# A layer with a 32-expert mixture on one core: expert results written from Pool's queue, token windows copied by VectorE one unit ahead, five experts instead of three with known addresses, four of them in pairs

## The chip, the core and the metric

The kernel runs on one core of a Trainium2 chip, as a single launch. The metric is the device time in microseconds (us) of that launch. A core has five engines that matter here: TensorE (PE in the rows, with its weight loads as PEld), VectorE (DVE), ScalarE (ACT), GpSimd (POOL) and SyncE (SP), which computes nothing and mainly issues DMAs. A q behind an engine's name (SPq, POOLq) is its sequencer, which waits, branches and issues. Each engine works through its own instructions in order and waits at semaphores for the others. DMAs move data between HBM and the on-chip memory; they run on 16 DMA engines that all queues share.

## What is computed

The reference is one layer over 512 latent tokens of width 1024: two mixers in parallel (a gated DeltaNet and a spatial gating MLP), an output projection with residual, and then the part that this change touches, a mixture of 32 experts. Each token picks one of four expert groups, and two of the eight experts in it:

```
p_group = jax.nn.softmax(t @ w_rg + b_rg)            # t: 512 tokens x 1024
grp = jnp.argmax(p_group, axis=-1)
logits_in = (t @ w_re + b_re) of the group grp       # 8 experts
top_p, top_i = lax.top_k(jax.nn.softmax(logits_in), 2)
...
hid = silu(t @ w1[e]) * (t @ w3[e])                   # 1024 x 256 each
out += (hid * gate[:, e]) @ w2[e]                     # 256 x 1024
```

The result is added to the residual and normalised. An expert has three parts of 1 MB each (float32, 128 x 2048): two hold w1 and w3, the third holds w2. All 32 experts are loaded, so 96 parts go through the DMA engines. There are 1024 assignments of a token to an expert, 32 for an expert in the mean. For the reference's inputs the router gives experts 0 to 4 these numbers of rows: 68, 9, 39, 31, 46; and the largest of the others 104, 94, 75, 65, 53, 47, 41, 35, 30.

## The kernel before, in words

The first 880 us compute the mixers and are not touched. Then come, for each block of 128 tokens, the output projection and the router's logits; `route` turns these into positions; `experts` runs the mixture; `combine` gathers each token's two results and writes the output.

**Routing.** `route` sorts the 1024 assignments by expert. It yields `off` (where an expert's rows begin), `count`, and a ranking of experts by count. Eight indirect DMAs on Pool's queue gather the token rows in that order (`xg`, 512 KB each, two in one buffer of 1 MB); TensorE transposes them into `xst` (ScalarE and VectorE copy the halves), 1024 columns of which are the sorted assignments. Of the experts, the first NS = 3 are taken by their number, so their addresses in HBM are known from the start. The other NR = 29 are taken by rank, the fullest first, and their addresses are read from `byi[0]`, which the ranking gives.

**Units.** `units` makes a list U. A unit is either one expert with a window of 128 columns of `xst`, or a pair of experts with 64 columns each; the two of a pair run side by side in TensorE, each on half of its columns. Before, U holds the three known experts singly, then the five largest singly, mixed with 12 pairs: 20 units. `unit_in` multiplies the window `exw` with w1 and w3 (`p<-eraw,exw`), forms `hid` with ScalarE and VectorE, and transposes it to `hT`. `unit_out` multiplies `hT` with w2 (`p<-eraw,hT`), VectorE scales the result into `ey`, and DMAs write its rows to `ysort` in HBM. They are issued in PIECES (rows 0 to 32 always, then 32 to 48, 48 to 64 and, for a single expert, 64 to 96 and 96 to 128 if the expert has as many rows).

**Conditional part.** A pair whose experts might have over 64 rows (ranks up to NB = 15) is followed by `second`: an `If` on all engines that repeats the unit for the rows past 64. There are five of them. The three parts of each of a pair's experts stay in their buffers until that `If` is done.

**Loads.** The list LOADS holds the parts in order of use: for each unit the first two parts of its experts, then the third parts of the unit before; the known experts come first. `load_parts(n)` issues loads on SP's queue up to number n. There are 16 buffers of 1 MB (8 in `er`, 8 in `er2`); the gathers `xg` use four of `er2`, so before routing at most 12 can be loaded. `route` is preceded by `load_parts(9)`, all that is known. Each buffer is used again when its part has been read.

**Queues.** SP issues, in order: the loads, the writes of `ey` pieces (L1198), and a register load for each condition (L1175). A DMA of one queue also waits until an earlier one, about eight DMAs back in the same queue, has landed. The window copy (L1152) stands on ScalarE just ahead of its `unit_in`. There are three `ey` buffers.

Of the kernel before, what the change touches and what calls it, by code (L numbers as in the profile page):

```python
# [9 lines left out]
F32 = mybir.dt.float32  # L10
F32R = mybir.dt.float32r
I32 = mybir.dt.int32
U32 = mybir.dt.uint32
AF = mybir.ActivationFunctionType
ALU = mybir.AluOpType
# [6 lines left out]
T = 512  # L22
# [8 lines left out]

NS, NB, NW = 3, 15, 5
NR = 32 - NS
NL = NR - NB
BASE = CAP * (NS + NB)
# [13 lines left out]
class K:  # L51
# [15 lines left out]
            mm(ps, wl(kt), xh(kt), start=False, stop=last and kt == kts - 1)  # L67


    ER, ER2, EY, HB = 8, 8, 3, 2  # L70

    PIECES, XL = ((0, 32), (32, 48), (48, 64), (64, 96), (96, 128)), (3,)

# [748 lines left out]
    def tail_mix(self, RM, R3):  # L822
# [58 lines left out]
        self.xst = self.xs.tile([128, KT, 2 * T + 64], F32, name="xst")  # L881
        R3.close()
        nc.gpsimd.memset(self.xst[:, :, 2 * T:], 0.0)
        self.load_parts(3 * NS)
        self.route(lg)

    def route_tiles(self):
# [31 lines left out]
    def route(self, lg):  # L919
# [116 lines left out]
        nc.gpsimd.tensor_tensor(end, self.off[0:1], win[0:1], op=SUB)  # L1036
        nc.gpsimd.tensor_tensor(end, end, self.count[0:1], op=ADD)
        nc.gpsimd.tensor_copy(self.cnti, end)
        by_rank(1, win[0:1, NS:])
        by_rank(2, end[:, NS:])  # L1040

# [24 lines left out]
    def moe_setup(self):  # L1066
        nc, c = self.nc, self.c
        BF = mybir.dt.bfloat16
        self.onesb = c.tile([128, 128], BF, name="onesb")
        nc.gpsimd.memset(self.onesb, 1.0)  # L1070
        self.lt = c.tile([128, 128], BF, name="lt")
        nc.gpsimd.affine_select(out=self.lt, in_=self.onesb, compare_op=ALU.is_gt, fill=0.0, base=0,
                                pattern=[[1, 128]], channel_multiplier=-1)

        self.tokn = c.tile([128, 2, 8], F32, name="tokn")
        for o, (pat, m) in enumerate((([[0, 8]], 1), ([[0, 2], [128, 4]], 0))):
            nc.gpsimd.iota(self.tokn[:, o], pattern=pat, base=0, channel_multiplier=m, allow_small_or_imprecise_dtypes=True)
        self.gate = c.tile([128, 2, 4], F32, name="gate")
        self.count = c.tile([128, 32], F32, name="count")
        self.off = c.tile([128, 32], F32, name="off")  # L1080
        self.offi = c.tile([1, 32], I32, name="offi")
        self.cnti = c.tile([1, 32], I32, name="cnti")
        self.byi = [c.tile([1, NR], I32, name=f"byi{i}") for i in range(3)]
        self.posi = c.tile([128, 8], I32, name="posi")
        self.tki = c.tile([128, 8], I32, name="tki")
        self.ysort = self.dp.tile([YROWS + 2 * T, D], F32, name="ysort")
# [22 lines left out]
    def units(self):  # L1109

        big = [(NS + r,) for r in range(NW)]
        small = [(NS + r, NS + r + 1) for r in range(NW, NR, 2)]
        self.U = [(e,) for e in range(NS)]
        while big or small:
            self.U += big[:1] + small[:2]
            big, small = big[1:], small[2:]

        ins = lambda u: [(e, k) for e in self.U[u] for k in range(2)]
        outs = lambda u: [(e, 2) for e in self.U[u]]
        self.LOADS = ins(0)  # L1120
        for u in range(1, len(self.U)):
            self.LOADS += ins(u) + outs(u - 1)
        self.LOADS += outs(len(self.U) - 1)
        self.LOADS.sort(key=lambda p: p[0] >= NS)
# [18 lines left out]
    def window(self, es, past=0):  # L1143

        nc = self.nc
        n = 128 // len(es)
        xw = self.eh.tile([128, KT, 128], F32, tag="exw", bufs=2, name="exw")
        for i, e in enumerate(es):
            src = self.offi[0:1, e:e + 1] if e < NS else self.byi[1][0:1, e - NS:e - NS + 1]
            o = nc.values_load(src, engines=(mybir.EngineType.Activation,), min_val=0, max_val=2 * T - 64,  # L1150
                               skip_runtime_bounds_check_because="the windows lie inside the tile")
            nc.scalar.copy(xw[:, :, n * i:n * i + n], self.xst[:, :, bass.ds(o + past, n)])  # L1152
        return xw

    def unit_in(self, es, w, xw):
# [17 lines left out]

    def rows_of(self, e):
        return self.nc.values_load(self.cnti[0:1, e:e + 1] if e < NS else self.byi[2][0:1, e - NS:e - NS + 1],  # L1175
                                   engines=(mybir.EngineType.SP,), min_val=0, max_val=2 * T,
                                   skip_runtime_bounds_check_because="an expert has at most T tokens")

    def unit_out(self, es, w2, hT, past=0):
        nc, ew = self.nc, self.ew  # L1180
        n = 128 // len(es)
        p2 = self.psm.tile([128, 2, 512], F32, tag="p2", bufs=2, name="p2")
        for h in range(2):
            for kt in range(2):
                for i in range(len(es)):
                    r = slice(n * i, n * i + n)
                    kw = {} if n == 128 else dict(tile_position=(0, n * i))
                    nc.tensor.matmul(p2[r, h, :], hT[:, kt, r], w2[i][:, kt, 512 * h:512 * h + 512],  # L1188
                                     start=kt == 0, stop=kt == 1, **kw)
        y = ew.tile([128, D], F32, tag="ey", bufs=self.EY, name="ey")  # L1190
        nc.vector.tensor_tensor(y, p2.rearrange("p a b -> p (a b)"), self.m5, op=MUL)  # L1191
        for i, e in enumerate(es):
            m = self.rows_of(e)
            row = CAP * e if e < NS + NB else BASE + 64 * (e - NS - NB)
            for a, b in self.PIECES:
                if past <= a < past + n:
                    kw = dict(cond=m > a) if a else {}
                    nc.sync.dma_start(self.ysort[row + a:row + b], y[n * i + a - past:n * i + b - past], **kw)  # L1198

    def second(self, es, w, w2):  # L1200

        src = self.byi[2][0:1, es[0] - NS:es[0] - NS + 1]
        m = self.nc.values_load(src, min_val=0, max_val=2 * T, skip_runtime_bounds_check_because="an expert has at most T tokens")
        with self.tc.If(m > 64):
            self.unit_out(es, w2, self.unit_in(es, w, self.window(es, 64)), 64)

    def experts(self):
        done, cur = 0, None
        for u in range(len(self.U) + 1):
            self.load_parts(done + self.ER + self.ER2)  # L1210
            last, cur = cur, None
            if u < len(self.U):
                es = self.U[u]
                w = [[self.eraw.pop((e, k)).rearrange("p (k c) -> p k c", k=4) for k in range(2)] for e in es]
                cur = es, w, self.unit_in(es, w, self.window(es) if u else self.xst[:, :, 0:128])
                done += 2 if len(es) == 1 else 0
            if last:
                es, w, hT = last
                w2 = [self.eraw.pop((e, 2)).rearrange("p (k c) -> p k c", k=2) for e in es]
                self.unit_out(es, w2, hT)  # L1220
                done += 1 if len(es) == 1 else 6
                if len(es) == 2 and es[0] < NS + NB:
                    self.second(es, w, w2)
# [270 lines left out]
```

## Time and profile before

| | us |
|---|---|
| three runs: median (lowest to highest) | 1249.03 (1247.0 to 1254.13) |
| the profiled execution, its own time | 1247.79 |
| its span, first to last instruction | 1246.1 |
| PE busy | 1055.2 (85%) |
| DVE busy | 593.1 (48%) |
| ACT busy | 429.6 (34%) |
| POOL busy | 218.8 (18%) |

The profiled execution lies 1.2 us below the median, and its span 1.7 us below its own time. The page's line of 40 slices shows PE at nine tenths over most of the span, at 4 tenths in the slice around the routing, and at nothing in the last. The DMA line reads 3 to 7 in the first two thirds and mostly 8 or 9 in the last third, where the experts are. To read the change, cut the span at 904 (routing), 924 (dynamic loads begin), 964, 1004 and 1204 us (the experts' end), and look in each stretch at what the DMA engines carry and at what SP's queue waits for.

### The profile page before, as it was taken

How to read it: one execution, taken by the hardware profiler on the slowest of the kernel's cores; microseconds unless marked ns; L12 is line 12 of the kernel's file. 1: busy time of each engine (PE TensorE's matmuls, PEld its weight loads, DVE VectorE, ACT ScalarE, POOL GpSimd, SP SyncE). 2: the span in 40 equal slices, each digit the busy share in tenths (PEclk: the TensorE clock that was granted, in tenths of full speed). 3: DMA queues.
4: the chain of work that ended last, by engine and by line, in shares of the span. 5: the costliest groups of instructions: out<-in, count | busy, mean ns of one | idle time of the engine just before them, and what ended most of it. 6: DMA issues, size and time to landing. Idle time of an engine off the chain costs nothing. (4 is left out here: it accounts for less than half of the span.)

```text
span 1246.1 us, 17491 instructions
## 1 busy us (share of the span) xinstructions
PE 1055.2 (85%) x6450; PEld 751.2 (60%) x6451; DVE 593.1 (48%) x1102; ACT 429.6 (34%) x850; POOL 218.8 (18%) x181
## 2 busy tenths in 40 slices
PE   4899878899798979988999999998859988889750
PEld 0577767787687768865677767887734332323210
DVE  5655774679365954585433434373571211111115
ACT  4656332754364535633235233242122001001002
POOL 2502111411141105111211011131150000000005
PEclk9999997899798989989999999998969998999985
DMA  9346652356322542336634457678569588999975
GB/s 372 94 155 230 185 181 57 106 137 236 85 97 79 172 115 86 90 115 189 237 105 149 154 172 267 199 235 319 213 225 412 201 325 350 376 367 400 406 297 219
DMA packets 108364, 262.01 MB, mean 210 GB/s; under 512 B 48400, under 2 KB 57072, under 8 KB 95600
## 3 DMA queue, kind: packets, MB, share of 16 engines
q1 hardware_dynamic: 99488, 238.45, 54.8%
q0 software_dynamic: 3456, 12.58, 2.7%
q10 hardware_dynamic: 5328, 9.77, 2.3%
q8 instruction: 54, 0.88, 0.3%
q14 instruction: 38, 0.31, 0.1%
HBM read 230.78 MB, written 47.30 MB: 223 GB/s over the span
## 5 line engine op out<-in xcount | busy, mean ns | idle before, releaser
L1163 PE MATMUL p<-eraw,exw 128*64 128x512 f32 (+1 forms) x496 | 150.5, 624 | 19.3 <-DMA eraw<-we 14.4
L63 PE MATMUL pcol<-xhi,wh 128*128 128x512 f32 x320 | 129.3, 404 | 3.5 <-ACT wh L121 3.2
L121 ACT CAST wh<-raw 128x1024 fp32r<-128x1024 f32 (+1 forms) x81 | 84.2, 1040 | 137.4 <-DMA raw<-win 34.1
L63 PE MATMUL pcol<-xhi,wl 128*128 128x512 f32 x320 | 128.4, 401 | 1.6 <-DVE wl L122 1.1
L63 PE MATMUL pcol<-xlo,wh 128*128 128x512 f32 x320 | 127.3, 398 | 0.0
L1163 PEld LDWEIGHTS p<-eraw,exw 128*64 128x64 f32 (+1 forms) x496 | 55.2, 155 | 104.5 <-issue 102.5
L122 POOL TENSOR_TENSOR wl<-raw,wh 128x1024 fp32r<-128x1024 f32 x27 | 65.7, 2434 | 276.2 <-ACT wh L121 216.1
L122 DVE TENSOR_TENSOR wl<-raw,wh 128x1024 fp32r<-128x1024 f32 (+1 forms) x54 | 66.6, 1233 | 58.5 <-ACT wh L121 50.8
L1188 PE MATMUL p<-eraw,hT 128*64 128x512 f32 (+1 forms) x256 | 84.5, 619 | 11.1 <-DMA eraw<-we 5.1
L63 PE MATMUL px<-xhi,wh 128*128 128x512 f32 x192 | 79.1, 412 | 9.4 <-DVE acc L349 6.5
L1165 ACT ACTIVATE hid<-p 128x256 f32<-128x256 f32 x20 | 7.7, 384 | 209.3 <-PE p L1163 206.8
L63 PE MATMUL px<-xhi,wl 128*128 128x512 f32 x192 | 77.4, 403 | 0.0
L63 PE MATMUL px<-xlo,wh 128*128 128x512 f32 x192 | 77.4, 403 | 0.0
L349 DVE SCALAR_TENSOR_TENSOR acc<-px,convw,acc 128x510 f32<-128x510 f32 (+1 forms) x96 | 71.4, 743 | 10.0 <-ACT acc L345 9.4
L63 PEld LDWEIGHTS pcol<-xhi,wh 128*128 128x128 f32 x320 | 60.8, 190 | 16.8 <-ACT wh L121 3.3
L63 PEld LDWEIGHTS pcol<-xhi,wl 128*128 128x128 f32 x320 | 60.8, 190 | 14.5 <-DVE wl L122 1.5
L63 PEld LDWEIGHTS pcol<-xlo,wh 128*128 128x128 f32 x320 | 61.1, 191 | 11.4
L1191 DVE TENSOR_TENSOR ey<-p,m5r 128x1024 f32<-128x1024 f32 x20 | 24.5, 1225 | 90.8 <-PE p L1188 60.6
L1166 DVE TENSOR_TENSOR hid<-hid,p 128x256 f32<-128x256 f32 x20 | 8.4, 421 | 115.1 <-ACT hid L1165 115.1
L1188 PEld LDWEIGHTS p<-eraw,hT 128*64 128x64 f32 (+1 forms) x256 | 27.3, 155 | 56.6 <-issue 46.1
L1321 POOL DMA_INDIRECT yk<-ysort,posi x8 | 8.2, 1019 | 288.5 <-SPq L1231 286.3
L483 DVE TENSOR_TENSOR xtmp<-X 112x30 f32<-112x30 f32 (+14 forms) x120 | 50.5, 421 | 11.4 <-POOL X L477 9.0
(394 smaller groups left out, 2171.2 us busy)
## 6 DMA issues: line engine op xcount, KB each, us to landing
eraw<-we SPq DMA_DIRECT2D x96, 1024.0 KB
raw<-win SPq DMA_DIRECT2D x64, 512.0 KB
adaw<-adaw SPq DMA_DIRECT2D x40, 512.0 KB
ysort<-wo SPq DMA_DIRECT2D x23, 512.0 KB
gr<-rowsd SPq DMA_DIRECT2D x8, 768.0 KB
ysort<-ey SPq DMA_DIRECT2D x48, 128.0 KB
adaw<-adaw POOLq DMA_DIRECT2D x8, 512.0 KB, 19.7
qd<-rowsd SPq DMA_DIRECT2D x8, 512.0 KB
```

The lines of the kernel that those rows point to most:

```text
L63: mm = lambda *a, **k: self.pace(self.nc.tensor.matmul(*a, **k))
L121: a = nc.scalar.copy(hi, src)
L122: b = (lo_eng or nc.vector).tensor_tensor(lo, src, hi.bitcast(F32), op=SUB)
L349: eng.scalar_tensor_tensor(acc[:, lo:hi], ps[:, lo + o:hi + o], w(d), acc[:, lo:hi], op0=MUL, op1=ADD)
L483: nc.vector.tensor_tensor(tv, bc(X[:, j + 1:, j], 2, j), bc(X[:, j, :j], 1, m), op=MUL)
L1163: nc.tensor.matmul(p13[r], xw[:, kt, r], w[i][kt // 4][:, kt % 4, :], start=kt == 0, stop=kt == KT - 1, **kw)
L1165: nc.scalar.activation(hid, p13[:, 0:256], AF.Silu)
L1166: nc.vector.tensor_tensor(hid, hid, p13[:, 256:512], op=MUL)
L1188: nc.tensor.matmul(p2[r, h, :], hT[:, kt, r], w2[i][:, kt, 512 * h:512 * h + 512], start=kt == 0, stop=kt == 1, **kw)
L1191: nc.vector.tensor_tensor(y, p2.rearrange("p a b -> p (a b)"), self.m5, op=MUL)
L1321: g = nc.gpsimd.indirect_dma_start(out=y[:, k, :], out_offset=None, in_=self.ysort, in_offset=bass.IndirectOffsetOnAxis(ap=self.posi[:, 4 ...
```

## The change

NS goes from 3 to 5, so 15 parts have known addresses. Experts 1 to 4 become two pairs, each followed by a conditional part, whose condition is the larger of the two counts (`mxi`, computed by VectorE). NR falls to 27, pairs by rank to 11; U has 19 units: 1 + 2 + 5 + 11, and there are seven conditional parts. `load_parts(12)` stands ahead of `route`. The writes of `ey` go from SP's queue to Pool's, with their register loads, and there are four `ey` buffers. The window copy goes from ScalarE to VectorE, and is issued for unit u + 1 behind `unit_in` of unit u.

```diff
-NS, NB, NW = 3, 15, 5
+NS, NB, NW = 5, 15, 5
-    ER, ER2, EY, HB = 8, 8, 3, 2
+    ER, ER2, EY, HB = 8, 8, 4, 2
...
-        self.load_parts(3 * NS)
+        self.load_parts(self.ER + self.ER2 - 4)
...
+        mx = rp.tile([1, NS - 1], F32, name="mxe")
+        nc.vector.tensor_tensor(mx, end[:, 0:NS - 1], end[:, 1:NS], op=ALU.max)
+        nc.vector.tensor_copy(self.mxi[:, 0:NS - 1], mx)
...
-        self.U = [(e,) for e in range(NS)]
+        self.U = [(0,)] + [(e, e + 1) for e in range(1, NS, 2)]
...
-            o = nc.values_load(src, engines=(mybir.EngineType.Activation,), min_val=0, max_val=2 * T - 64,
+            o = nc.values_load(src, engines=(mybir.EngineType.DVE,), min_val=0, max_val=2 * T - 64,
-            nc.scalar.copy(xw[:, :, n * i:n * i + n], self.xst[:, :, bass.ds(o + past, n)])
+            nc.vector.tensor_copy(xw[:, :, n * i:n * i + n], self.xst[:, :, bass.ds(o + past, n)])
...
-                                   engines=(mybir.EngineType.SP,), min_val=0, max_val=2 * T,
+                                   engines=(mybir.EngineType.Pool,), min_val=0, max_val=2 * T,
...
-                    nc.sync.dma_start(self.ysort[row + a:row + b], y[n * i + a - past:n * i + b - past], **kw)
+                    nc.gpsimd.dma_start(self.ysort[row + a:row + b], y[n * i + a - past:n * i + b - past], **kw)
...
-        src = self.byi[2][0:1, es[0] - NS:es[0] - NS + 1]
+        src = self.mxi[0:1, es[0]:es[0] + 1] if es[0] < NS else self.byi[2][0:1, es[0] - NS:es[0] - NS + 1]
...
-                cur = es, w, self.unit_in(es, w, self.window(es) if u else self.xst[:, :, 0:128])
+                cur = es, w, self.unit_in(es, w, xw)
+                if u + 1 < len(self.U):
+                    xw = self.window(self.U[u + 1])
```

SP's queue around the routing, before. L874 writes the rows that the gathers read; L1133 are loads with a known address, L1138 those with an address from the ranking:

```order
L1133 DMA eraw<-we 128x2048 x6
L874 DMA h2d<-x_7413 128x1024
L836 DMA x_7693<-x 128x1024
L874 DMA h2d<-x_7415 128x1024
L874 DMA h2d<-x_7417 128x1024
L1133 DMA eraw<-we 128x2048
L874 DMA h2d<-x_7693 128x1024
L1136 TENSOR_LOAD byi_103
L1138 ISA
L1138 DMA eraw<-we 128x2048
```

The same place now (a load with a known address is L1138, one by rank L1143):

```order
L1138 DMA eraw<-we 128x2048 x6
L874 DMA h2d<-x_7413 128x1024
L836 DMA x_7693<-x 128x1024
L874 DMA h2d<-x_7415 128x1024
L874 DMA h2d<-x_7417 128x1024
L1138 DMA eraw<-we 128x2048 x4
L874 DMA h2d<-x_7693 128x1024
L1138 DMA eraw<-we 128x2048 x3
L1141 TENSOR_LOAD byi_104
L1143 ISA
L1143 DMA eraw<-we 128x2048
```

Three more loads stand ahead of the last `h2d` write, and three more with known addresses ahead of the ranking's first use.

SP's queue in the middle of the experts, before: two loads of one unit, then the first of another unit's writes with the register load for their conditions.

```order
L1136 TENSOR_LOAD byi_103
L1138 ISA
L1138 DMA eraw<-we 128x2048
L1138 ISA
L1138 DMA eraw<-we 128x2048
L1198 DMA ysort<-ey 32x1024
L1175 TENSOR_LOAD byi_105
L1198 ISA
L1198 DMA ysort<-ey 16x1024
```

A load that comes later in this queue stands behind all of these writes. SP's queue around the first conditional part now (L1208 loads its condition, L1209 branches):

```order
L1143 DMA eraw<-we 128x2048
L1208 TENSOR_LOAD mxi
L1209 COMPARE_AND_BRANCH
L1209 UNCONDITIONAL_BRANCH x2
L1141 TENSOR_LOAD byi_104
L1143 ISA
L1143 DMA eraw<-we 128x2048
```

And Pool's queue for the second pair now, where before it held only the register loads and branches of the five conditional parts:

```order
L1203 DMA ysort<-ey 32x1024
L1180 TENSOR_LOAD cnti
L1203 ISA
L1203 DMA ysort<-ey 16x1024
L1203 ISA
L1203 DMA ysort<-ey 16x1024
L1203 DMA ysort<-ey 32x1024
L1180 TENSOR_LOAD cnti
L1203 ISA
L1203 DMA ysort<-ey 16x1024
```

The writes have left SP's queue altogether, body of the `If` included; between two loads there stands at most a register load and a branch.

## Rows read from the trace of the kernel before

**Rows 1.** Busy time by stretch: start:end, us, engines (x instructions), PEclk, DMA share, GB/s
```profile
core 0: us, PE busy (x) PEld busy (x) DVE busy (x) ACT busy (x) POOL busy (x), PEclk, DMA share, GB/s
904.00:916.00 12.00, 2.69 (x76) 2.40 (x76) 9.39 (x25) 1.70 (x5) 4.69 (x8) 0.50 0.11 45
924.00:964.00 40.00, 38.17 (x124) 19.98 (x123) 13.04 (x27) 9.85 (x15) 4.42 (x8) 0.96 1.01 414
964.00:1004.00 40.00, 38.71 (x140) 13.85 (x139) 8.81 (x12) 3.35 (x6) 0.00 (x0) 1.00 0.57 194
1004.00:1204.00 200.00, 166.31 (x594) 59.56 (x592) 27.30 (x41) 19.78 (x37) 0.00 (x0) 0.95 0.95 382
```
**Rows 2.** SP's waits, 924 to 1214: waiter <- releaser: us, times, longest
```profile
SPq L1138 <- DMA eraw<-we: 50.9, 25, 3.3
SPq L1198 <- DMA ysort<-ey: 33.5, 22, 3.2
SPq L1198 <- DMA eraw<-we: 29.7, 15, 2.6
```
**Rows 3.** SP's queue in order of time: start, us, line, DMA, count
```profile
896.11 0.33 SPq L1133 DMA_DIRECT2D eraw<-we  x1
...
986.67 0.37 SPq L1138 DMA_DIRECT2D eraw<-we  x1
987.92 10.89 SPq L1198 DMA_DIRECT2D ysort<-ey  x11
1000.32 3.90 SPq L1138 DMA_DIRECT2D eraw<-we  x6
```
**Rows 4.** PE in order of time, 937 to 975: start, us, line, tiles, [idle before]
```profile
937.06 1.94 PE L1031 MATMUL pxt<-ident,xg 128*128 128x128 f32 x8 [0.89 <-DMA xg<-h2d,tki]
...
943.06 13.90 PE L1163 MATMUL p<-eraw,exw 128*128 128x512 f32 x32
...
963.88 3.60 PE L1188 MATMUL p<-eraw,hT 128*128 128x512 f32 x8
...
967.63 7.08 PE L1163 MATMUL p<-eraw,exw 128*64 128x512 f32 x30
```
**Rows 5.** DMA by queue, 916 to 924: Pool's queue: packets, MB, share of the DMA engines
```profile
q0 software_dynamic: 619, 2.28, 87.3%
```
**Rows 6.** The same, 924 to 964
```profile
q0 software_dynamic: 533, 1.91, 12.3%
```
**Rows 7.** PE's waits, 938 to 1206
```profile
PE p L1163 <- DMA eraw<-we: 14.4, 5, 3.9
...
PE p L1188 <- DVEq L1204: 1.3, 1, 1.3
```
**Rows 8.** Pool in order of time, 2 to 8: eight plain DMAs that it issues
```profile
2.61 4.45 POOL L129 DMA_DIRECT2D adaw<-adaw  x8
```
**Rows 9.** Pool in order of time, 914 to 927: two of eight gathers that it issues
```profile
914.61 1.03 POOL L1027 DMA_INDIRECT xg<-h2d,tki  x1 [1.58 <-DVE e L1000]
...
918.46 1.73 POOL L1027 DMA_INDIRECT xg<-h2d,tki  x1 [0.30 <-issue]
```
**Rows 10.** Pool in order of time, 1210 to 1226: the first result gather
```profile
1215.41 1.00 POOL L1321 DMA_INDIRECT yk<-ysort,posi  x1 [286.32 <-SPq L1231]
```
**Rows 11.** Tile exw: the window copies on ScalarE (ns min/median/max, first and last)
```profile
L1152 ACT COPY exw<-xst x31: 613/619/1053, 940.4 to 1164.1; 128x512 f32 x24, 128x1024 f32 x7
```
**Rows 12.** DVE in order of time: an operation with one tensor in and one out
```profile
1240.15 0.48 DVE L1336 TENSOR_SCALAR yk<-xst,fss 128x512 f32<-128x512 f32 x1
```
**Rows 13.** SP's queue in order of time at the experts' end
```profile
1184.16 6.14 SPq L1138 DMA_DIRECT2D eraw<-we  x4
...
1193.04 20.51 SPq L1198 DMA_DIRECT2D ysort<-ey  x24
```
**Rows 14.** PE in order of time: the last unit's second layer
```profile
1200.79 3.65 PE L1188 MATMUL p<-eraw,hT 128*64 128x512 f32 x16 [1.28 <-DVE hT L1171]
```
**Rows 15.** DVE in order of time: the last unit's scaling
```profile
1206.31 1.23 DVE L1191 TENSOR_TENSOR ey<-p,m5r 128x1024 f32<-128x1024 f32 x1 [5.57 <-DMA ysort<-ey]
```

More of the change, by code (lines that the diff above doesn't have):

```diff
@@ L1082, in moe_setup @@
         self.cnti = c.tile([1, 32], I32, name="cnti")
+        self.mxi = c.tile([1, NS - 1], I32, name="mxi")
         self.byi = [c.tile([1, NR], I32, name=f"byi{i}") for i in range(3)]
@@ L1207, in experts @@
     def experts(self):
-        done, cur = 0, None
+        done, cur, xw = 0, None, self.xst[:, :, 0:128]
         for u in range(len(self.U) + 1):
```

## The prediction

> **What bounds the kernel now.** I read the busy time by stretch first, since the change touches only what lies behind the routing. In the last 200 us of the experts the DMA engines are 95% busy at 382 GB/s, and PE, busy 166 of 200 us, waits for loads [rows 1, 7]: there the end is set by when the 96 parts have come in. Two stretches fall out of this. From 904 to 916, while VectorE routes, the DMA engines are at a share of 0.11, because all that has a known address is already loaded [rows 1]. And from 964 to 1004 they are at 0.57 and 194 GB/s with PE at 97% [rows 1]: single units use three parts in a first layer of 13.90/2 = 6.95 us and a second of 3.60 [rows 4], so they free 3 MB in 10.6 us, less than the DMA engines could carry, and SP's queue is held as well.
>
> SP's own waits tell the second half. In 290 us it waits 50.9 us in its loads for earlier loads, which costs nothing, since eight are then under way; but it waits 33.5 + 29.7 us in the writes of results for other DMAs to land [rows 2], and each load behind them waits too. At 987.92 eleven writes hold the queue for 10.89 us, and the next loads start at 1000.32 [rows 3].
>
> The idle DMA time from 924 to 1204 is 0.43 x 40 = 17.2 us in the second stretch and 0.05 x 200 = 10 us in the last, together 27.2 us. What they move in these 280 us is 0.414 x 40 + 0.194 x 40 + 0.382 x 200 = 100.7 MB, in 252.8 busy us: 0.398 MB per us, or 2.63 us for a part of 1.05 MB.
>
> **Part by part.** *Loads ahead of the routing.* Twelve parts instead of nine are issued where the ninth is issued now, at 896.11 [rows 3]. Three parts are 7.9 us of DMA time, and run in a stretch that is nearly idle: they are gone from the later sum, -7.9 us. The last row block's write for the gathers stands behind them in SP's queue; four parts from 896 end by some 907, and the gathers start only at 914.6 [rows 9], so I count no delay (0 to +3).
>
> *Known addresses for parts 13 to 15.* Before, three loads join the gathers at 924. Now they are loaded already, and those that follow need the gathers' buffers. The gathers alone ran at 2.28 MB in 8 us; with the loads beside them the last 1.91 MB took some 13 us, and TensorE has the last at 937.06 [rows 4 to 6]. At the first rate they take 6.7 us; one load shares with them, so I take 932, 5 us sooner. The first pair's window copies and matmuls then start near 937.5 instead of 943.06 [rows 4].
>
> *Two pairs in place of four singles.* A pair's first layer takes 7.08 us [rows 4], no more than a single's, so one unit of 10.6 us of PE is saved, and each unit frees six parts. But the pairs are conditional, and their six buffers come free only behind the `If`. From 937.5: two first layers, the second pair's beside the first's, 14.2; a second layer 3.6; the transposes and the branch, for which PE waited 1.3 once [rows 7]. The `If` is done near 957. Until then the DMA engines have the rest of the gathers and seven parts (the 13th to the 19th), 1.9 + 7.3 MB, 22 us at 0.414 from 924: they stop near 946 and stand for 11 us. From 957 on, six to nine buffers are free at once and a unit of PE (11 us) frees as much as 15.7 us of loads fill, so I see no further stop. The counts given for experts 1 to 4 are at most 46, so neither conditional part runs.
>
> *Writes on Pool's queue.* No load stands behind a write any more, and none waits in the `If` for writes to land. That is most of the 10 us in the last stretch; I leave 3 us (0 to 10). So idle time falls from 27.2 to 11 + 3 = 14 us: -13.2 us. Pool has 13 pairs with six pieces and six singles with five, 108 in all. An issue costs 4.45/8 = 0.56 us plain [rows 8], up to 1.73 + 0.30 beside VectorE's work [rows 9]. I take 1.3, between them: 8 us for a pair, whose loads take 15.7. It is hidden, except at the end.
>
> *Window copies on VectorE.* 31 copies, at most 1.05 us each on ScalarE [rows 11] and 0.96 on VectorE (twice 0.48, [rows 12]), on an engine busy 27 of 200 us [rows 1], a unit before they are needed: 0. What queues behind one there is the scaling of the unit before; its results have a unit's time.
>
> *The end.* From the last unit's second layer at 1200.79 to the first result gather at 1215.41 [rows 10, 14] lie 14.6 us: the matmuls 3.65, VectorE's wait for an `ey` buffer until 1206.31 [rows 15], 1.23, and 7.9 for SP's last writes, 24 of which took 20.51 us behind the last loads [rows 13]. With Pool the wait for a buffer is gone (-1.9), but the last two units' pieces are issued at 0.56 to 2.0 us each, and the gather stands behind them on the same engine: 12 pieces at 1.3 are 15.6 us, of which some 8 lie behind the last scaling. I take 0, with -4 and +4 as bounds.
>
> Sum: -7.9 - 13.2 + 0 = -21.1 us. Against the profiled execution's own 1247.8 us this gives 1226.7, which I round to **1227**. The median of the three runs is 1.2 us above that execution.
>
> **A rule that speaks against it.** A gather's issue on Pool stretched from 1.03 to 1.73 us once while VectorE worked beside it [rows 9]. The Trainium skill, page "SBUF — State Buffer", section "SBUF: two separate sides", says that a DMA issued from GpSimd's queue has its descriptors written by GpSimd, which VectorE locks out while it copies float32 within SBUF; the same page gives 620 ns alone and about 3100 ns beside such a copy, and the change brings both together. If every piece took 3.1 us, a pair would need 18.6 us of Pool, more than its loads, which is the rival below; the row's stretch of 0.7 us, and one unit's copies of at most 1.05 us, would leave it hidden.
>
> **The rivals.** *The bound moves back to the buffers (0.18).* Seven conditional parts keep twelve parts each from being overwritten; if the DMA engines stop before each `If` as they do before the first, the idle time stays at 27 us and only the three early loads count: 1240. For it: PE has just 34 us of idle time in 200 [rows 1]. Against: a unit's six buffers are 15.7 us of loads, and PE needs 11.
>
> *More is won (0.12).* No idle time after the first `If`, and loads at the 0.414 of the full stretch [rows 1] rather than 0.398: 97.5 MB take 235.5 instead of 245 us; with 3 us less idle this is 1214.
>
> *Pool becomes the bound (0.07), slower than before.* Its 108 pieces lie between 940 and the last part's landing near 1180. From 2.2 us a piece on they take longer than that, and the `ey` buffers pass the wait on to VectorE and PE. The row's worst is 2.03; with 0.6 us for the branch's and the register loads' share it is 2.6: 281 us, to 1221, and with 2 us to land, 30.7 from the first gather to the span's end and 1.7 around it 1256.
>
> *The change doesn't do what it says (0.03).* If the twelve loads delay the gathers by the 8 us that they take, the gain in the routing is given back: about 1235, and with the buffers' rival no change.
>
> **How the numbers follow.** The forecast has the remaining 0.60. A measurement tells about 0.5% from no change, so faster means below 1242.8. The forecast's own range is 1217 to 1235; it reaches to 1211 for the rival above it in gain, with the end at -4, and to 1243 for the buffers' rival with some more idle time. Faster: 0.60 + 0.12 + two thirds of 0.18 + 0.02 = 0.86. Same: 0.06 + 0.01 = 0.07. Slower: 0.07.
>
> **What would show it.** Twelve loads by 898 and a DMA share well over 0.11 from 904 to 908; the last gather transposed near 932; a gap in the DMA engines from about 946 to 957 and hardly another until the last part, near 1179; SP waiting for loads and buffers only; Pool busy under 10 us per unit; 14 to 15 us from the last second layer to the first result gather. The prediction is wrong if the DMA share past 960 stays under 0.95 (then the buffers or Pool hold it: the waits of SP for PE, or of VectorE for writes, tell which), if the gathers start later than 916, or if Pool's pieces take over 2 us.

## The result, and the profile after

The changed kernel takes 1215.32 us (median of four runs, 1214.53 to 1216.37), where the kernel before, run beside it, takes 1248.01: a ratio of 0.9732, 95% interval 0.9694 to 0.9769, so 2.3 to 3.1% faster. The profiled execution takes 1215.9 us with a span of 1214.3, 31.8 us less than the span before. The forecast was 1227, with 1217 to 1235 as its own range and 1211 to 1243 with the rivals: the sign held, the time lies below the forecast's own range and inside the wider one. 11 to 12 us more were won than its sum says, almost exactly what the rival "more is won" gave.

Busy time by stretch, columns as in [rows 1]:

```profile
904.00:916.00 12.00, 2.44 (x74) 2.18 (x73) 6.73 (x19) 1.87 (x5) 6.31 (x8) 0.50 0.54 205
924.00:964.00 40.00, 38.30 (x165) 17.89 (x164) 15.86 (x35) 5.75 (x10) 6.83 (x16) 1.00 0.68 258
950.00:961.00 11.00, 10.70 (x46) 4.39 (x43) 2.08 (x4) 0.38 (x1) 0.00 (x0) 1.00 0.02 7
964.00:1004.00 40.00, 39.40 (x145) 14.24 (x145) 8.76 (x15) 1.54 (x4) 6.51 (x19) 1.00 1.01 418
1004.00:1172.00 168.00, 148.74 (x542) 49.43 (x540) 34.42 (x57) 4.61 (x12) 19.61 (x73) 0.98 1.01 421
```

The stretch of the routing now carries 205 GB/s instead of 45. There is one full stop, from 950 to 961 (7 GB/s), and behind it none at all: where [rows 1] has 194 and 382 GB/s, there are 418 and 421. SP's waits from 904 to 1200 (waiter <- releaser: us, times, longest) and its queue in order of time (start, us, line, DMA, count):

```profile
SPq L1143 <- DMA eraw<-we: 87.5, 47, 3.0
SPq L1143 <- PEq L1209: 59.6, 7, 17.7
```

```profile
894.63 2.13 SPq L1138 DMA_DIRECT2D eraw<-we  x4
909.31 0.33 SPq L874 DMA_DIRECT2D h2d<-x  x1
922.13 11.73 SPq L1138 DMA_DIRECT2D eraw<-we  x3
936.90 211.72 SPq L1143 DMA_DIRECT2D eraw<-we  x81
```

From 937 to 1149 SP issues loads and nothing else. It waits for earlier loads to land, with a full queue behind it, and 59.6 us at seven `If`s, but only the first of these, 17.7 us, leaves the DMA engines without work. The waits in the writes of [rows 2], 33.5 and 29.7 us, are gone. Pool in order of time: the pieces of the first pair (start, us, line, DMA, [idle before]), and the group of all 108 pieces (busy us, mean ns):

```profile
961.28 0.50 POOL L1203 DMA_DIRECT2D ysort<-ey  x1 [15.01 <-DVE ey L1196]
961.98 0.04 POOL L1203 DMA_DIRECT2D ysort<-ey  x1 [0.21 <-DMA ysort<-ey]
962.40 0.04 POOL L1203 DMA_DIRECT2D ysort<-ey  x1 [0.38 <-DMA ysort<-ey]
963.30 0.49 POOL L1203 DMA_DIRECT2D ysort<-ey  x1 [0.85 <-issue]
964.46 0.49 POOL L1203 DMA_DIRECT2D ysort<-ey  x2 [0.67 <-issue]
```

```profile
L1203 POOL DMA_DIRECT2D ysort<-ey x108 | 30.5, 287 | 219.0 <-DVE ey L1196 164.7 <-DVEq L1209 23.2 <-issue 17.1
```

A piece that is written takes 0.49 us, one that its condition skips 0.04; a pair's six are through in 3.7 us, and ahead of the pieces Pool is idle for 219 us. PE around the last gathers and the first pair:

```profile
934.85 2.02 PE L1031 MATMUL pxt<-ident,xg 128*128 128x128 f32 x16 [0.25 <-DVE xst L1033]
937.34 3.70 PE L1193 MATMUL p<-eraw,hT 128*128 128x512 f32 x8 [0.47 <-DVE xst L1033]
940.97 13.95 PE L1168 MATMUL p<-eraw,exw 128*64 128x512 f32 x62
...
960.39 7.11 PE L1168 MATMUL p<-eraw,exw 128*128 128x512 f32 x16 [0.30 <-PEq L1209]
```

The end, on PE and on Pool; these answer [rows 14, 10]:

```profile
1169.53 3.65 PE L1193 MATMUL p<-eraw,hT 128*64 128x512 f32 x16 [1.28 <-DVE hT L1176]
```

```profile
1174.77 0.49 POOL L1203 DMA_DIRECT2D ysort<-ey  x1 [2.52 <-DVEq L1238]
...
1182.31 1.01 POOL L1328 DMA_INDIRECT yk<-ysort,posi  x1 [4.72 <-issue]
```

The last second layer starts 31.3 us earlier than before (1169.53 against 1200.79), and the first result gather follows it by 12.8 us, not 14.6.

### The profile page after: what moved, and what is told of

The parts are those of the page before. It is cut to its first block, busy times and chain, and to the rows that moved or that the text cites. A ratio compares the mean times of both kernels' runs of the same rounds, so it can differ in the third digit from the quotient of the medians.

```text
span 1214.3 us, 17472 instructions
## 1 busy us (share of the span) xinstructions
PE 1040.8 (86%) x6448; PEld 740.3 (61%) x6449; DVE 601.6 (50%) x1132; ACT 408.9 (34%) x818; POOL 250.5 (21%) x289
## 5 line engine op out<-in xcount | busy, mean ns | idle before, releaser
L1168 PE MATMUL p<-eraw,exw 128*64 128x512 f32 (+1 forms) x496 | 142.4, 611 | 14.1 <-DMA eraw<-we 12.0
L1168 PEld LDWEIGHTS p<-eraw,exw 128*64 128x64 f32 (+1 forms) x496 | 47.0, 148 | 99.3 <-issue 81.3
L1193 PE MATMUL p<-eraw,hT 128*64 128x512 f32 (+1 forms) x256 | 76.6, 599 | 1.9 <-DVE hT L1176 1.3
L1203 POOL DMA_DIRECT2D ysort<-ey x108 | 30.5, 287 | 219.0 <-DVE ey L1196 164.7
L63 PE MATMUL pbr<-bhi,wl 128*128 128x512 f32 x128 | 50.2, 394 | 0.3 <-DVE wl L122 0.3
L63 PE MATMUL pbr<-bhi,wh 128*128 128x512 f32 x128 | 49.9, 390 | 0.0
```

Of the source, the lines that this page charges most:

```text
L63: mm = lambda *a, **k: self.pace(self.nc.tensor.matmul(*a, **k))
L1168: nc.tensor.matmul(p13[r], xw[:, kt, r], w[i][kt // 4][:, kt % 4, :], start=kt == 0, stop=kt == KT - 1, **kw)
L1203: nc.gpsimd.dma_start(self.ysort[row + a:row + b], y[n * i + a - past:n * i + b - past], **kw)
```

## The experiments

Up to the loads ahead of the routing the code is the same in all kernels, yet the first gather of the routing starts anywhere between 908.2 and 929.5 us in these executions. So beside each median stands the time from that gather's start to the end of the span of the profiled execution, 331.5 us before (1246.1 - 914.61) and 300.7 after (1214.3 - 913.57). Ratios are to the kernel before, run beside each one. Each figure of the last column comes from one profiled execution.

| kernel | median us | ratio, 95% | first gather to end, us |
|---|---|---|---|
| before | 1248.01 | 1 | 331.5 |
| changed | 1215.32 | 0.9732 (0.9694 to 0.9769) | 300.7 |
| changed, again (e9) | 1219.25 | 0.9767 (0.9733 to 0.98) | 300.4 |
| writes back on SP (e1) | 1251.33 | 0.9987 (0.9962 to 1.0013) | 336.2 |
| nine loads early (e2) | 1220.09 | 0.9739 (0.9701 to 0.9777) | 303.8 |
| five single units (e3) | 1229.24 | 0.9801 (0.9773 to 0.9829) | 312.9 |
| no `If` of the first pairs (e4) | 1212.09 | 0.9666 (0.9638 to 0.9694) | 295.2 |
| before, with writes on Pool (e5) | 1225.69 | 0.9824 (0.9769 to 0.9879) | 306.8 |
| each piece written twice (e6) | 1235.59 | 0.9899 (0.9846 to 0.9952) | 317.9 |
| second halves behind the last unit (e7) | 1210.29 | 0.9689 (0.963 to 0.9747) | 296.1 |
| the same, pairs before singles (e8) | 1217.47 | 0.9738 (0.9677 to 0.9799) | 295.0 |
| window copies by ScalarE, in place (e10) | 1216.31 | 0.9732 (0.9682 to 0.9781) | 301.1 |
| more copies beside the pieces (e11) | 1216.39 | 0.9742 (0.9711 to 0.9773) | 300.3 |
| e7, rows of the end in other buffers (e12) | 1207.24 | 0.9663 (0.9639 to 0.9686) | 288.8 |

**e9, the changed kernel again.** It tells how far the column on the right can be trusted: 300.4 against 300.7 us, while the two medians, measured at different times, are 4 us apart. A second profile exists of this kernel alone.

> The changed kernel again, unchanged, beside the runs of this call. Both theories: from the first gather of the routing to the end 300 to 302 us, as in its first profile (300.7); its time as far below the kernel before as there, 2.3 to 3.1%.

**e1, the writes back in SP's queue**, with the register loads for their conditions.

```diff
-                                   engines=(mybir.EngineType.Pool,), min_val=0, max_val=2 * T,
+                                   engines=(mybir.EngineType.SP,), min_val=0, max_val=2 * T,
...
-                    nc.gpsimd.dma_start(self.ysort[row + a:row + b], ...
+                    nc.sync.dma_start(self.ysort[row + a:row + b], ...
```

> The changed kernel, with the writes of results put back into SP's queue (the branch that Pool evaluated goes back with them). Theory: the 11 us that the result has over the forecast, and most of the idle time that went, come from the loads no longer standing behind writes. From 1004 to 1172 the changed kernel moves 168 us x 421 GB/s = 70.7 MB; at the 382 GB/s of the kernel before that takes 185 us, so the run should be about 17 us slower than the changed kernel, 1228 to 1236 us, with SP waiting over 40 us in line 1203 for other DMAs and the DMA engines under 400 GB/s after 1004. Rival: the rate comes from the pairs and the loads of known addresses; then the writes' queue is worth under 5 us, 1215 to 1220, and the DMA engines stay at 415 to 421 GB/s.

Measured: the whole gain is gone, 1251.33 us; from the first gather 336.2, so the edit is worth 35.5 us (by the ratios, 0.9987 against 0.9732, some 32). Busy time by stretch and SP's waits from 936 to 1200 in this kernel:

```profile
964.00:1004.00 40.00, 34.36 (x124) 12.26 (x122) 7.26 (x14) 1.15 (x3) 0.00 (x0) 0.96 0.79 308
1004.00:1172.00 168.00, 135.38 (x452) 45.32 (x451) 31.50 (x54) 4.21 (x11) 0.00 (x0) 0.92 0.89 354
```

```profile
SPq L1203 <- DMA eraw<-we: 39.4, 20, 3.2
SPq L1203 <- DMA ysort<-ey: 38.5, 21, 3.4
...
SPq L1209 <- SPq L1209: 18.0, 16, 5.0
```

SP waits 78 us in line 1203 with the next loads behind it, and the DMA engines fall from 421 to 354 GB/s. The theory's mechanism holds, but its time is missed: its 17 us were half of the price. The rival is out. All other parts of the change together, without this one, win nothing: the ratio is 0.9987, and from the first gather it is even 4.7 us more (336.2 against 331.5). What the earlier loads and the pairs bring with the writes on Pool (e2, e3) does not show without it. SP's 18.0 us at the `If`s, where it now evaluates the pieces' conditions too, may be a part of that; no run separates it.

**e5, the same edit alone, in the kernel before.**

> The kernel before, with only the writes of results moved to Pool's queue (three experts of known address as units of their own, nine parts early, the places copied by ScalarE). Theory: this is most of the change. The run with writes on SP lost 33 us or more against the changed kernel, the five singles 12 us; three singles lie between those and the pairs, so this kernel should be 20 to 28 us faster than the kernel before, 1224 to 1232 us where that runs at 1252, with the DMA engines at 415 to 421 GB/s after 1010. Rival (the forecast's step): the writes give 13.2 us alone, 1236 to 1241.

The diff is e1's, reversed. Measured: 24.7 us less from the first gather, 23.1 by the medians. The forecast's 13.2 is out. (The profiled execution is the slowest of five, 1237.89 us; its first gather starts at 929.54, 15 us later than in the kernel before, so its stretches are 15 us later too.) Busy time by stretch:

```profile
976.00:1011.00 35.00, 33.71 (x127) 11.88 (x127) 7.58 (x11) 3.36 (x6) 5.67 (x19) 1.00 0.67 241
1011.00:1180.00 169.00, 152.69 (x554) 56.11 (x552) 26.16 (x39) 19.59 (x36) 20.50 (x77) 0.97 1.01 421
```

Behind 1011 the DMA engines run full, without pairs of known address and without earlier loads. What is left of the loss lies from 976 to 1011, where PE is busy for 33.71 of 35 us with the second layers of the single units and the first two pairs, up to the first `If`. This kernel has three `ey` buffers; no run takes the fourth by itself.

**e6, every piece written twice.**

```diff
+        self.ydup = self.dp.tile([YROWS + 2 * T, D], F32, name="ydup")
...
                     nc.gpsimd.dma_start(self.ysort[row + a:row + b], ...
+                    nc.gpsimd.dma_start(self.ydup[row + a:row + b], ...
```

> The changed kernel with each piece of the results written a second time, from Pool's queue, to a place in memory that nobody reads. Theory: the 421 GB/s of the DMA engines are for all queues together, and after 961 these engines set the pace, so the 6.3 MB of Pool's queue a second time cost their 15 us: 1228 to 1234, with 421 GB/s as before and Pool's pieces still under 1 us. Rival A: writes go beside the loads at no cost, 0 to 4 us, with more than 425 GB/s in all. Rival B: Pool becomes the bound with 216 pieces; then VectorE waits for results to be written, TensorE for buffers, and the DMA share after 1004 falls under 0.95, over 20 us slower.

Measured: 17.2 us more from the first gather, 2 us over the price of the bytes. DMA by queue from 1004 to 1154 (packets, MB, share of the DMA engines), the changed kernel first, then this one:

```profile
q1 hardware_dynamic: 8177, 59.58, 95.2%
q0 software_dynamic: 1395, 3.55, 6.0%
```

```profile
q1 hardware_dynamic: 7698, 56.06, 89.2%
q0 software_dynamic: 2780, 7.11, 12.0%
```

Pool's queue moves twice as much, 3.56 MB more, and SP's 3.52 MB less: the 422 GB/s are one budget for both. So writes on Pool's queue are not free beside loads, and Pool does not hide their bytes; what the move took away is the standing still. The theory holds, both rivals are out.

**e2, nine loads ahead of the routing instead of twelve.**

```diff
-        self.load_parts(self.ER + self.ER2 - 4)
+        self.load_parts(9)
```

> The changed kernel with nine parts loaded ahead of the routing instead of twelve. Theory (the forecast's step): three parts are 7.9 us of DMA time in a stretch that is nearly idle, so the run should be 5 to 9 us slower than the changed kernel, 1220 to 1224. Rival: the DMA engines stand from 950 to 961 because all buffers are full until the first If; three parts that come later only fill this gap, so the run is 0 to 3 us slower, 1215 to 1218, with the gap at 4 us or less.

Measured: 3.1 us more from the first gather; its median is 0.8 and 4.8 us above the changed kernel's two, and the ratios (0.9739 against 0.9732 and 0.9767) tell no difference. Between the theory and the rival, and for another reason than either gave. The stretches of this kernel, and the second of them in the changed kernel:

```profile
904.00:916.00 12.00, 2.69 (x76) 2.41 (x76) 9.60 (x26) 1.05 (x3) 4.99 (x7) 0.50 0.61 216
916.00:924.00 8.00, 1.94 (x8) 1.57 (x8) 6.45 (x17) 1.21 (x4) 6.45 (x6) 0.50 1.01 392
955.00:965.00 10.00, 9.70 (x43) 3.96 (x40) 1.57 (x3) 0.38 (x1) 0.00 (x0) 1.00 0.04 15
```

```profile
916.00:924.00 8.00, 5.84 (x19) 4.34 (x20) 6.55 (x16) 1.17 (x2) 6.32 (x6) 0.50 0.88 311
```

With five experts of known address the three parts need no routing, wherever they are issued: undone, they move by some 8 us, still into its shadow, and share the DMA engines with the gathers. The price is the gathers' delay: the first pair's first layer starts 30.2 us after the first gather (945.49 - 915.27) instead of 27.4, and all else follows by as much. The stop at the first `If` stays.

**e3, experts 1 to 4 as four units.**

```diff
-        self.U = [(0,)] + [(e, e + 1) for e in range(1, NS, 2)]
+        self.U = [(e,) for e in range(NS)]
```

> The changed kernel with experts 1 to 4 as four units of their own instead of two pairs, so without the two Ifs and with two more units of 10.6 us on TensorE. Theory: the pairs' gap of 11 us in the DMA engines stands for what singles lose by freeing 3 MB in 10.6 us (0.28 MB per us against 0.42, 11 to 14 us over four units), so the run is within 3 us of the changed kernel, 1212 to 1218, with no full stop at 950 and a share of 0.65 to 0.8 from 950 to 990. Rival: the pairs are where the gain over the forecast lies; then 10 to 17 us slower, 1225 to 1232.

Measured: 12.2 us more from the first gather. The theory is out: singles lose more than the pairs' stop of 11 us. Two stretches:

```profile
964.00:1010.00 46.00, 46.00 (x140) 18.33 (x140) 12.91 (x20) 1.54 (x4) 5.30 (x24) 1.00 0.69 267
1004.00:1154.00 150.00, 141.44 (x503) 48.51 (x502) 33.89 (x58) 4.61 (x12) 20.13 (x68) 0.99 0.96 394
```

PE is busy for all of the 46 us while the DMA engines move 267 GB/s, and its two more units (21 us) still show after 1004, with 394 GB/s against 422. The pairs are worth their 12 us by sparing PE, which is the bound there.

**e4, no `If` for the first two pairs**, so that tokens past the 64th of experts 1 to 4 are left out.

```diff
-                if len(es) == 2 and es[0] < NS + NB:
+                if len(es) == 2 and NS <= es[0] < NS + NB:
                     self.second(es, w, w2)
```

> The changed kernel with the conditional second half of the two first pairs left out (it computes the tokens past the 64th of experts 1 to 4, and does not run for these counts). Theory: the stop of the DMA engines from 950 to 961 is only the wait for the If; without it the first layer of unit 1 frees four buffers near 955 and the loads go on 6 to 9 us sooner, so the run is 5 to 9 us faster than the changed kernel, 1206 to 1210. Rival: TensorE, busy 39.4 of 40 us from 964 to 1004, is late by as much, so the loads only stop somewhere later: 0 to 2 us, 1213 to 1216.

Measured: 5.5 us less from the first gather, at the low end of the theory's 5 to 9. But the stop has not gone, it has moved:

```profile
940.00:991.00 51.00, 51.00 (x192) 17.62 (x192) 13.45 (x24) 1.53 (x4) 7.56 (x22) 1.00 1.00 410
991.00:1002.00 11.00, 10.70 (x39) 3.95 (x36) 2.83 (x5) 0.38 (x1) 2.09 (x7) 1.00 0.48 172
```

**e7, all second halves behind the last unit.** Every pair then frees its buffers when its matmuls are done; a tail, skipped for these counts, loads the weights again if any count of a pair is over 64.

```diff
...
+    def late(self):
...
+        with self.tc.If(load(self.mxi[0:1, 0:1], 0, 2 * T) > 64):
+            for es in [es for es in self.U if len(es) == 2 and es[0] < NS + NB]:
...
+                if u == len(self.U):
+                    self.late()
                 done += 1 if len(es) == 1 else 6
-                if len(es) == 2 and es[0] < NS + NB:
+                if False:
                     self.second(es, w, w2)
```

> The changed kernel with the conditional second halves of all pairs moved behind the last unit, where they load their weights again, under one condition for all of them; it computes the same for all inputs. Without the first two Ifs the DMA engines stopped from 992 to 1002 instead of 950 to 961. Theory: that second stop is TensorE's (busy 20.0 of 20 us from 964 to 984, all buffers full, a single unit that frees three parts), so taking the other Ifs away too gives 0 to 2 us over the run without the first two: 1210 to 1213. Rival: it is the first If behind them, and goes with it: 5 to 8 us faster than that run, 1204 to 1207.

My theory fell: the second stop was the next `If`'s, not TensorE's, and it goes with it. The DMA engines run full from 936 on, and the last second layer starts 245.8 us after the first gather (1160.83 - 915.03) instead of 256.0. The end gives 4.4 us back, by Pool's row and SP's:

```profile
936.00:1154.00 218.00, 209.07 (x768) 72.61 (x770) 51.57 (x89) 8.57 (x21) 28.02 (x96) 0.98 1.01 419
```

```profile
1177.99 1.00 POOL L1346 DMA_INDIRECT yk<-ysort,posi  x1 [9.14 <-DMA xst<-x1d]
```

```profile
1166.00 2.89 SPq L1336 DMA_DIRECT2D xst<-x1d  x3
```

The rows that the end adds are loaded over the tokens, which the tail may still read, so these loads wait behind its `If`, until 1166 instead of 1150, and the first gather of results waits for them.

**e8, e7 with two pairs ahead of each single unit.**

```diff
-            self.U += big[:1] + small[:2]
+            self.U += small[:2] + big[:1]
```

> The kernel of the run before this one, with two pairs ahead of each single unit instead of behind it. Theory: the stop near 992 comes from a single unit that takes TensorE 10.6 us and frees three parts, 3.1 MB, where the DMA engines could load 4.5 MB, while all buffers are full; two pairs ahead of it, which free six parts each, draw the stock down first, so it goes: 4 to 8 us faster than the run before, 1203 to 1208, with a DMA share of 1.0 from 940 on. Rival: the stop only moves to the next single: within 2 us of it.

Within 1.1 us of e7 from the first gather (295.0 against 296.1; the medians say slower, with intervals that overlap). The expectation fell with e7's theory: no stop was left for the order to remove.

**e12, e7 with the rows of the end in three of the weights' buffers**, loaded ahead of the condition.

```diff
+                    self.combine_load()
                     self.late()
...
-        row = self.xst.rearrange("p k t -> p (k t)")
-        self.xs4 = [row[:, D * n:D * n + D] for n in range(4)]
+        two = [self.eraw_tile("res").rearrange("p (k d) -> p k d", k=2) for i in range(3)]
+        self.xs4 = [two[n // 2][:, n % 2] for n in range(4)]
...
-        self.combine_load()
```

> The kernel with all second halves behind the last unit, and with the rows that the end adds (four row blocks and the last gain) loaded into three of the weights' buffers instead of over the tokens, so that they need not wait behind the condition. In that kernel the first gather of results waited 9.14 us for these loads and started 17.2 us after the last second layer, against 12.8 in the changed kernel. Theory: this gives back the 4.4 us: 291 to 293 us from the first gather of the routing to the end, against 300.7 of the changed kernel and 296.1; 1204 to 1208 where the changed kernel has 1215. Rival: the gather waits for Pool's pieces and the branch instead, 295 to 297.

Measured: 1207.24 us, 12 us less than the changed kernel run beside it (1219.25), with intervals that don't touch; from the first gather 288.8, less than expected. It is the fastest of all. But the expected 4.4 us did not come where they were expected: the first result gather follows the last second layer by 15.8 us (1171.67 - 1155.85), against 17.2 in e7 and 12.8 in the changed kernel. Of the 7.3 us against e7 the other 6 lie ahead of that layer (3.7) and behind that gather (2.3), and no run tells why. For these counts its tail is skipped, as the conditional halves are in the other kernels, so its price when taken was not measured. From 924 until the loads end there is no stop:

```profile
924.00:1154.00 230.00, 219.83 (x832) 78.68 (x830) 57.40 (x108) 11.90 (x26) 31.97 (x103) 1.00 1.01 417
```

**e10, the places copied by ScalarE and where they are used.**

```diff
-            nc.vector.tensor_copy(xw[:, :, n * i:n * i + n], ...
+            nc.scalar.copy(xw[:, :, n * i:n * i + n], ...
...
-                cur = es, w, self.unit_in(es, w, xw)
-                if u + 1 < len(self.U):
-                    xw = self.window(self.U[u + 1])
+                cur = es, w, self.unit_in(es, w, self.window(es) if u else self.xst[:, :, 0:128])
```

> The changed kernel with the places copied by ScalarE and where they are used, as in the kernel before. Theory (the forecast's step): 0, within 2 us of the changed kernel, as ScalarE has time and its copies are at most 1.05 us each; from the first gather to the end 299 to 303 us. Rival: with the DMA engines full, the copies stand on TensorE's path in each unit; then 19 units by up to 0.5 us, 5 to 10 us slower.

301.1 us against 300.4 of the changed kernel run beside it: no difference, as the forecast has it.

**e11, 3.4 us of further copies on VectorE after each unit's scaling**, whose results nobody reads.

```diff
+        for q in range(8):
+            junk = ew.tile([128, 512], F32, tag="junk", bufs=1, name="junk")
+            nc.vector.tensor_copy(junk, self.xst[:, q % 8, 0:512])
         for i, e in enumerate(es):
             m = self.rows_of(e)
```

> The changed kernel with eight more float32 copies of 128x512 within SBUF on VectorE after the scaling of each unit's results, 3.4 us of copies beside the pieces that Pool writes; they go to a tile that nobody reads. Theory: pieces keep their 0.49 to 0.59 us, or stretch to at most the 1.65 us of the gathers beside VectorE's work; Pool has 15 us per pair, so the time is 0 to 3 us above the changed kernel. Rival (the forecast's third, by Pool's lock): pieces take 2 us and more, the six of a pair over 12 us, and the run is 5 us slower or more.

Measured: 300.3 us from the first gather, no difference. VectorE and Pool in one place, and the group of all 108 pieces of this kernel:

```profile
1070.10 5.96 DVE L1199 COPY junk<-xst 128x512 f32<-128x512 f32 x13
```

```profile
1068.77 0.50 POOL L1206 DMA_DIRECT2D ysort<-ey  x1 [12.12 <-DVEq L1212]
...
1070.45 0.63 POOL L1206 DMA_DIRECT2D ysort<-ey  x1 [0.52 <-issue]
...
L1206 POOL DMA_DIRECT2D ysort<-ey x108 | 32.1, 302 | 217.5 <-DVE ey L1196 151.3 <-DVEq L1212 23.8 <-issue 16.2
```

The piece issued at 1070.45, amid thirteen copies, takes 0.63 us instead of 0.49; over all pieces the mean goes from 287 to 302 ns. Not every piece met a copy, since some of the copies stand elsewhere on VectorE: of the 58 that are written, 20 overlap one in the trace, and those take 0.59 us in the mean and 0.72 at most. That is a stretch of one or two tenths of a microsecond, not of two whole ones. These are Pool's times for a piece; when each landed, the trace does not show.

## Why the prediction was right, and where its sum was off

Right were the sign, where the DMA engines' time would come back, and the one stop at the first `If`. That the time lies inside the wide range owes something to luck: the range had been drawn down to 1211 for the rival "more is won", to which the forecast gave 0.12, and it is that rival's time that came.

**The rate, the term that was mis-sized.** The forecast took the share of the DMA engines and their rate apart: idle time 27.2 us, and 0.398 MB per us while busy, and let the change act on the first alone. The idle time came out as it said: the share is 0.68 for the 40 us from 924 and full behind them, so 0.32 x 40 = 12.8 us, against 14. But 0.398 was no property of the DMA engines; a full stretch has 0.421 (1004 to 1172 above), and 0.414 already stood in [rows 1] from 924 to 964. By that rate the 100.7 MB before need 239 us of 280, so 41 us were lost, not 27.2; after, 0.258 x 40 + 0.418 x 40 + 0.421 x 168 = 97.8 MB need 232 of 248, so 16 us. The term of -13.2 is -25. Runs e1 and e5 show what carries most of it: the writes' queue alone is 24.7 us in the kernel before and 35.5 in the changed one. Where SP stands in writes, engines that count as busy move less: e1 has 354 GB/s at a share of 0.89, which is 398 at a full one, against 417 in the changed kernel (421 / 1.01). That this is because few loads are then left under way is argued, not shown. What the runs take away one at a time (35.5, 12.2 for the pairs in e3, 3.1 in e2) is more than the whole of 30.8 us: each is worth its price only with the others in place.

**"More is won"** (0.12) named this: no stop after the first `If`, and the rate of a full stretch. It gave 1214, without a cause for the rate; e1 and e5 supply one. The trace spoke for it more than I allowed, since a full stretch was in [rows 1] to be seen; I took the mean for the price of a part because it came from more bytes.

**Loads ahead of the routing** (-7.9). That DMA time was used: 205 GB/s from 904 to 916, and the bytes behind 924 fall by 2.9 MB, 7 us at 0.421 (by construction, 25 and 7 make up the 32 us between the two windows of 280 and 248 us). But e2 shows that the early place itself carries only 3.1 us; the rest then lies with the known addresses, which no run took away alone. The step gave all to one edit. The gathers were not delayed: they start at 913.57, before at 914.61, and in both kernels the last thing that Pool waits for there is VectorE ("<-DVE e L1000", 1.03 and 1.58 us), not the write behind the loads.

**The last gathers** (5 us sooner). The first layer behind them starts 27.4 us after the first gather, before 28.45 (943.06 - 914.61): 1.1 us sooner. The step failed on what comes last there. PE waited only 0.89 us for the last gather ([rows 4]), and its own work, the transpositions and unit 0, fills the time. PE from its first transposition to the first layer of the next unit (stretch, us, busy, PEclk, DMA share, GB/s), before and after:

```profile
919.40:943.06 23.66, 21.83 (x90) 0.84 1.00 390
917.91:940.97 23.06, 21.40 (x90) 0.87 0.91 334
```

With 21.83 of 23.66 us busy, gathers that land 5 us sooner could bring little more than the one us that came. After, PE's last waits there are for VectorE's copies of the transposed blocks ("<-DVE xst", 0.25 and 0.47).

**The pairs.** The `If` ends at 960.1, the forecast said 957, and the DMA engines stand for 11 us, from 950 to 961 instead of 946 to 957; no other stop follows, as it said. What the stop costs is less than its length: without the first two `If`s 5.5 us come back (e4), and nearly all of it only when no `If` holds buffers (in e7 the last second layer is 10.2 us sooner). The buffers' rival (0.18) was right that conditional parts are what stops the loads, and wrong that it would happen at each, where SP's waits (59.6 us at seven `If`s) cost the DMA engines nothing behind the first. It also counts twelve parts held by each condition, where a pair has six. Six parts, freed by a unit, are 15 us of DMA time, more than a unit of PE.

**Pool.** Expected 1.3 us a piece, measured 0.49 or 0.04; the rival (0.07) that it becomes the bound is far off, as Pool is idle for 219 us and busy with pieces for 30.5. (Its own sum gives 1255, not 1256; and two of the eight gathers before were long, 1.73 and 1.58 us, not one.) The rule of the Trainium skill, page "SBUF — State Buffer", section "SBUF: two separate sides", that VectorE's float32 copies within SBUF lock GpSimd out of writing descriptors (620 ns alone, about 3100 ns beside a copy) is not borne out here: 0.49 us apart from copies, 0.63 amid thirteen of them and 0.72 at most (e11). The measurement decides.

**Window copies** (0): e10 shows 0. **The end** (0, from -4 to +4): -1.8, the `ey` wait of [rows 15] is gone, and behind the last scaling Pool's pieces take 2.8 us (1174.77 to 1177.59), not 8. From the first result gather to the end it takes 32.0 us, before 30.7, so that 0.5 of the 1.8 are left.

**That the loads delay the gathers** (0.03): not seen.

## What to carry to other kernels

Where transfers set the pace, take the bytes of a stretch against the rate of a full stretch of the same trace, and count all of the difference as lost; a busy share of 0.95 can hide a tenth (382 against 421 GB/s). A queue that feeds the bound should carry nothing that waits: here moving 108 small conditional writes off it was most of the gain, and the rest of the change was worth nothing without it. Pool's was the only other queue that was tried. A condition behind which buffers come free holds the loads even if it is never true, so put the rare part last, with its own loads, and see that nothing else at the end waits behind it; what such a tail costs when it is taken was not measured here.

## What the runs showed of the hardware

- The 421 to 422 GB/s of the DMA engines are shared one to one by a queue of large reads and one of small writes (3.56 MB more of one, 3.52 MB less of the other in 150 us), with no loss by the mixture.
- A DMA that Pool skips by its condition takes 0.04 us, with 0.38 to 0.85 us until the next; one that is issued takes 0.49 us, and 0.63 beside copies on VectorE. The gathers, on the same engine, take 0.94 to 1.66 us in the changed kernel's routing; no run tells what makes some of them longer.
- An `If` that isn't taken costs PE 0.30 us (the wait ahead of 960.39), but the buffers that it would read stay held until then: SP stands 17.7 us at the first.
